# Deferred sums in the seven-product blocks, gate rows behind them, and an early start of the last projection in a two-layer trunk kernel

## The chip, the core and the metric

The kernel runs on one core of one Trainium2 chip. The metric is the time of one execution in microseconds (us). Before the change it is 1751.2 us, the median of three runs (1747.75 to 1752.89).

The core has a matrix engine (TensorE, PE in the rows), a vector engine (VectorE, DVE), a scalar engine (ScalarE, ACT), a general engine (GpSimd, POOL), and a queue engine that issues transfers (SyncE, SP). Each works through its own list of instructions in order and waits where an operand or a buffer isn't ready.

## What is computed

Two layers over 512 tokens of 2048 features, all in float32. Layer 0 is an attention layer; the change touches nothing in it. Layer 1 is an mLSTM with 8 heads (q and k of 128, v of 256 features a head):

```python
proj = x @ w_in
qk, v, o, gates, z = jnp.split(proj, [o1, o2, o3, o4], axis=-1)
qk = silu(causal_depthwise_conv(qk, conv_w, conv_b))     # 4 taps
q, k = jnp.split(qk, 2, axis=-1)
i_pre, f_pre = split(gates + gate_b)                      # 8 + 8 columns
cell = mlstm_chunkwise(q, k, v, i_pre, f_pre)             # decays from cumulated log-sigmoid(f), running maximum
cell = rmsnorm(cell, head_norm)                           # per head
y = (sigmoid(o) * cell * silu(z)) @ w_out
x = layernorm(ALPHA * x + y, ln_w, ln_b)
```

## The kernel before

Every float32 product is three products of rounded parts: hi·hi, hi·lo and lo·hi (`mm3`). A weight tile comes by a transfer of SyncE into `raw` (a ring of 3), ScalarE casts it to `whi` (L169), VectorE subtracts to get `wlo` (L170). A matmul covers 128 x 128 x 512; 24 of them use up one pair of K tiles. So VectorE must end one subtraction for each such group, or TensorE waits.

The order is written by a small planner in the program itself: `tick`, called between groups of products, runs tasks (generators) whose due time on a clock of counted TensorE work has passed; a `yield n` puts a task off by n us. `finish` drains a task at once. The framework then fixes the order on each engine.

Layer 1 goes through these stages:

- `values_out` for columns 0 to 511 of v: tokens 0 and 1, then 2 and 3 while the rest of the layer's input is still being transposed ("late").
- `gates` (L740 onward): one load of the 16 gate columns, 32 products, then `gate_rows`: a run of small VectorE operations on 8 partitions (log-sigmoid as a series, a reciprocal, running sums and maxima, L761 to L795), and after a pause a transpose of the rows. Their results are the cells' decays (`self.R` in DRAM) and gate columns (`self.gt`).
- `values_out` for columns 1536 to 2047, and beside it the task `mlstm_combos` (L917, with L281 to L284 and splits): eight bursts that build the sums of input tiles which the seven-product blocks need.
- Five `quad` blocks: each computes a 2 x 2 block product with seven products instead of eight. Phase 1 takes products q1 and q5 (96 matmuls), phase 2 q7, q6, q3 (144), phase 3 q2 and q4 (96); weights of several products are sums (L348, L360, L362, L381). After phase 2 ten sums over results follow (L368 to L374), after phase 3 four (L386). The first quad gives v columns 512 to 1535, each other one the columns of o and z of two heads, of which sigmoid(o)·silu(z) goes to `ascr` in DRAM. Phases alternate between the two sets of four accumulators, `acc` and `ps`.
- Four pairs of heads: v of the pair (`v_block`), the q and k products (`gemm_b`), convolution and SiLU (`conv_silu`, L808 to L811), and two `cell` tasks of one head each: decay loads on GpSimd's queue, exp, mask, S = k·q, scaled and split; products with v; root mean square (with L262 on GpSimd); scaling (L878); transposes; the result goes to `gscr` in DRAM, for the last two heads it stays.
- `out_proj` with w_out: blocks of 512 columns, residual tiles (`resid1`: `n1` times LayerNorm row plus bias on GpSimd, L1071 and L1072), statistics, and `finish1`, the last LayerNorm. One cell runs at a time (`width` 1), beside whatever products come.

A cell takes up to 13 tiles of the `t` pool (16), and the residual tiles of a block 4 more of it.

Of the kernel before, what the change touches and what calls it, by code (L numbers as in the profile page):

```python
# [2 lines left out]

# [13 lines left out]
P = 128  # L17
# [63 lines left out]
class Kern:  # L81
    def __init__(self, ctx, tc):
# [12 lines left out]
        self.banks = self.ps, self.acc  # L95

# [132 lines left out]
    def gemm_a(self, w, col0, x, toks, last=1):  # L229


        nk = len(x)
        out = {tb: self.acc() for tb in toks}
        units = []
        for k0 in range(0, nk, 2):
# [14 lines left out]
            for i, tb in enumerate(toks):  # L250
                s = slice(tb * P, (tb + 1) * P)
                for kk, (xh, xl), wk in units:
                    self.mm3(out[tb], (xh[:, s], xl[:, s]), wk, kk == 0, kk == nk - 1)
                self.tick()
# [20 lines left out]
    def combos(self, te, to, alloc):  # L275
# [14 lines left out]
        return out  # L290

    def quad(self, w, c0, c1, x, S, done):
# [48 lines left out]
        for i in range(0, n, 2):  # L341
# [8 lines left out]
            mul(q5, so, 1, i, taken2(t[-1]))  # L350
        e1, e5 = two(self.t), two(self.t)
# [356 lines left out]
    def out_proj(self, w_out, g, resid, finish, last=1):  # L708
# [7 lines left out]
        blocks = [((0, 1, 2, 3), 0), ((0, 1, 2, 3), 1)] + [(p, c) for p in ((0, 1), (2, 3)) for c in (2, 3)]  # L716
        for toks, cb in blocks:
            for tb in toks:
                t = r[tb, cb] = self.t()
                resid(tb, cb, t)  # L720
            out = self.gemm_a(w_out, cb * 512, g, toks, last if toks[0] == 2 and cb == 3 else 1)
            for tb in toks:
                t = r[tb, cb]
                nc.vector.scalar_tensor_tensor(t, t, ALPHA, out[tb], op0=ALU.mult, op1=ALU.add)
                nc.vector.bn_stats(stats[tb][:, cb], t)
            if cb == 3:
                moments = {}
                for tb in toks:
                    mv, a = self.small(2, 4), self.small()
                    nc.vector.bn_aggr(mv, stats[tb])  # L730
                    nc.vector.tensor_scalar(a, mv[:, 1:2], EPS, None, ALU.add)
# [389 lines left out]
```

## Time and profile before

| what | us |
|---|---|
| median of three runs | 1751.2 |
| profiled execution | 1744.94 |
| its span (first to last instruction) | 1743.2 |
| TensorE busy | 1629.5 (93%) |
| VectorE busy | 1095.0 (63%) |
| ScalarE busy | 742.3 (43%) |
| GpSimd busy | 151.2 (9%) |

The mean clock granted to TensorE in this execution was 0.979 of full speed. By stretch of the span:

| stretch, us | what runs | TensorE busy, us |
|---|---|---|
| 722 to 770 | first values, late transposes | 48.00 of 48 |
| 770 to 782 | gates | 9.48 of 12 |
| 782 to 825 | last values, gate rows, combos | 43.00 of 43 |
| 825 to 850 | first quad's head | 4.91 of 25 |
| 848 to 1271 | five quads | 393.51 of 423 |
| 1271 to 1471 | pair projections with cells 0 to 3 | 199.66 of 200 |
| 1471 to 1589 | cells 4 to 7, first block of the last projection | 79.41 of 118 |
| 1589 to 1743 | rest of the last projection, LayerNorm | 138.51 of 154 |

A busy share is an average over stages with different limits: where TensorE is full, another engine's work costs nothing; where it isn't, the row says which wait ended last. Busy time at a lower clock counts as busy, so the granted clock stands beside it.

### The profile page before, as it was taken

How to read it: one execution, taken by the hardware profiler on the slowest of the kernel's cores; microseconds unless marked ns; L12 is line 12 of the kernel's file. 1: busy time of each engine (PE TensorE's matmuls, PEld its weight loads, DVE VectorE, ACT ScalarE, POOL GpSimd, SP SyncE). 2: the span in 40 equal slices, each digit the busy share in tenths (PEclk: the TensorE clock that was granted, in tenths of full speed). 3: DMA queues.
4: the chain of work that ended last, by engine and by line, in shares of the span. 5: the costliest groups of instructions: out<-in, count | busy, mean ns of one | idle time of the engine just before them, and what ended most of it. 6: DMA issues, size and time to landing. Idle time of an engine off the chain costs nothing.

```text
span 1743.2 us, 20540 instructions
## 1 busy us (share of the span) xinstructions
PE 1629.5 (93%) x7466; PEld 1338.5 (77%) x7466; DVE 1095.0 (63%) x1880; ACT 742.3 (43%) x1178; POOL 151.2 (9%) x238
## 2 busy tenths in 40 slices
PE   8999999999999999999599998998899998679996
PEld 7888888888888888778477776876688887457875
DVE  3374222777778346859876877786756564555477
ACT  3343223545555224452434444544545564653232
POOL 1000000000000001101000000000110111324300
PEclk9999999999999999999799999999999999789999
DMA  7333333322222546664455475547655743456454
GB/s 207 107 96 97 97 97 85 91 63 66 73 70 88 157 145 218 214 174 87 135 133 161 121 149 108 175 120 145 135 149 123 145 122 121 122 159 207 155 193 169
DMA packets 172134, 230.05 MB, mean 132 GB/s; under 512 B 23593, under 2 KB 93321, under 8 KB 172033
## 3 DMA queue, kind: packets, MB, share of 16 engines
q1 hardware_dynamic: 157872, 195.72, 41.9%
q0 software_dynamic: 7248, 20.44, 3.9%
q10 hardware_dynamic: 6912, 12.59, 2.4%
q8 instruction: 58, 0.95, 0.2%
q14 instruction: 44, 0.35, 0.1%
HBM read 206.51 MB, written 19.96 MB: 130 GB/s over the span
## 4 chain that ended last, share of the span: by engine, by line
PE 68%; DVE 14%; DMA 12%; ACT 3%; issue 3%; POOL 0%; SPq 0%; DVEq 0%; POOLq 0%; ACTq 0%
PE acc L204 56%; PE ps L204 10%; DMA raw<-in_ml_w_in_dram 8%; DVE wlo L170 5%; PE ps L201 2%; DMA raw<-in_ml_w_out_dram 2%; ACT whi L169 1%; DVE raw L360 1%; DVE t L381 1%; DVE h L170 1%; DMA e<-in_ml_w_in_dram 1%; DVE e L917 0%; DMA e<-vscr 0%; ACT h L169 0%; DVE t L372 0%
## 5 line engine op out<-in xcount | busy, mean ns | idle before, releaser
L170 DVE TENSOR_TENSOR wlo<-raw,whi 128x1024 fp32r<-128x1024 f32 (+1 forms) x311 | 377.3, 1215 | 324.3 <-ACT whi L169 311.0
L169 ACT CAST whi<-raw 128x1024 fp32r<-128x1024 f32 (+1 forms) x315 | 324.3, 1030 | 570.6 <-PE acc L204 376.9
L204 PE MATMUL acc<-whi,h 128*128 128x512 f32 x1656 | 533.3, 396 | 15.2 <-ACT whi L169 8.6
L204 PE MATMUL acc<-h,whi 128*128 128x512 f32 x1536 | 473.7, 393 | 2.5 <-DVE whi L170 2.5
L204 PEld LDWEIGHTS acc<-whi,h 128*128 128x128 f32 x1656 | 313.2, 189 | 81.0 <-ACT whi L169 10.0
L204 PE MATMUL acc<-wlo,h 128*128 128x512 f32 x828 | 327.0, 395 | 14.1 <-DVE wlo L170 14.1
L204 PEld LDWEIGHTS acc<-h,whi 128*128 128x128 f32 x1536 | 286.8, 189 | 60.7 <-DVE whi L170 2.9
L204 PE MATMUL acc<-h,wlo 128*128 128x512 f32 x736 | 287.5, 391 | 0.0
L204 PEld LDWEIGHTS acc<-wlo,h 128*128 128x128 f32 x828 | 157.0, 190 | 51.7 <-DVE wlo L170 20.9
L204 PEld LDWEIGHTS acc<-h,wlo 128*128 128x128 f32 x736 | 138.4, 188 | 29.5
L204 PE MATMUL ps<-whi,h 128*128 128x512 f32 x488 | 156.3, 392 | 0.0
L204 PE MATMUL ps<-wlo,h 128*128 128x512 f32 x244 | 97.1, 398 | 12.6 <-DVE wlo L170 12.6
L204 PEld LDWEIGHTS ps<-whi,h 128*128 128x128 f32 x488 | 92.1, 189 | 19.1
L169 ACT CAST whi<-t 128x512 fp32r<-128x512 f32 x120 | 69.1, 617 | 59.6 <-PE ps L204 34.4
L204 PE MATMUL acc<-whi,v 128*128 128x512 f32 x248 | 84.4, 399 | 0.0
L201 PE MATMUL ps<-ident,t 128*128 128x128 f32 x352 | 60.1, 288 | 22.6 <-ACT t L878 16.9
L170 DVE TENSOR_TENSOR wlo<-t,whi 128x512 fp32r<-128x512 f32 x120 | 77.9, 685 | 1.1 <-ACT whi L169 0.9
L201 PEld LDWEIGHTS ps<-ident,t 128*128 128x128 f32 x352 | 46.0, 147 | 38.1 <-ACT t L878 19.8
L204 PEld LDWEIGHTS ps<-wlo,h 128*128 128x128 f32 x244 | 45.9, 188 | 28.2 <-DVE wlo L170 19.0
L204 PE MATMUL ps<-h,h 128*128 128x128 f32 (+3 forms) x288 | 62.0, 328 | 0.1
L685 ACT ACTIVATE t<-ps,s 128x128 f32<-128x128 f32 (+3 forms) x64 | 33.7, 527 | 65.2 <-DVE s L684 65.1
L204 PE MATMUL ps<-whi,v 128*128 128x512 f32 x120 | 42.4, 409 | 20.1 <-ACT whi L169 20.1
(209 smaller groups left out, 1740.0 us busy)
## 6 DMA issues: line engine op xcount, KB each, us to landing
raw<-in_ml_w_in_dram SPq DMA_DIRECT2D x136, 512.0 KB, 4.9
raw<-in_mla_w_in_dram SPq DMA_DIRECT2D x48, 512.0 KB, 3.8
raw<-in_mla_w_out_dram SPq DMA_DIRECT2D x48, 512.0 KB, 3.8
raw<-in_ml_w_out_dram SPq DMA_DIRECT2D x48, 512.0 KB, 4.5
e<-in_ml_w_in_dram SPq DMA_DIRECT2D x40, 256.0 KB, 4.8
t<-in_x_dram SPq DMA_DIRECT2D x16, 256.0 KB, 6.5
raw<-in_mla_w_kvb_dram SPq DMA_DIRECT2D x16, 256.0 KB, 3.3
raw<-in_mla_w_kvb_dram SPq DMA_DIRECT2D x32, 128.0 KB, 2.4
```

What stands on the lines that cost most here:

```text
L169: a = self.nc.scalar.copy(hi, src)
L170: b = self.nc.vector.tensor_tensor(lo, src, hi.bitcast(F32), op=ALU.subtract)
L201: self.nc.tensor.transpose(out, in_, ident)
L204: self.nc.tensor.matmul(out, lhsT, rhs, start=start, stop=stop)
L360: V.tensor_tensor(w12, w12, w22, op=ALU.add)
L381: V.tensor_tensor(t[i // 2][j], t[i // 2][j], half(w21, j), op=ALU.add)
L685: nc.scalar.activation(pt[bi], s[:, :n], AF.Exp, bias=b, scale=scale, accum_out=tot)
```

## The change

Four edits. Of the sums over results in `quad`, all but the first two (L368) aren't issued where they were but put into a list, `self.pending`; `some(2)` takes two entries after each step of phases 1 and 3, so those of phase 2 fall into the first three steps of phase 3, those of phase 3 into the first two steps of the next quad's phase 1. `gates` and its rows are called behind the five quads, and a cell starts only when the rows are done. `v_block` is called for each head, within the cell, with hi and lo in one tile. `out_proj` goes over blocks 0 and 1 twice: first K tiles 0 to 11 (heads 0 to 5), then 12 to 15, added with four more evictions a block; the residual tiles of these blocks come from `h`, and its residual and LayerNorm loads are issued from SyncE instead of ScalarE. Pauses in `cell` are longer.

```diff
+    def some(self, n):
+
+        for _ in range(min(n, len(self.pending))):
+            self.pending.pop(0)()
...
             mul(q1, xe, 0, i, taken(w11))
             mul(q5, so, 1, i, taken2(t[-1]))
+            self.some(2)
...
-        for m in range(2):
+
+        def sums(m):
             V.tensor_tensor(e5[m], e5[m], u[m], op=ALU.subtract)
             V.tensor_tensor(u[m], u[m], q7[m], op=ALU.add)
+
+        def upper(m):
             V.tensor_tensor(c12[m], e5[m], q3[m], op=ALU.add)
             done(m, 1, c12[m])
+
+        def lower(m):
             V.tensor_tensor(e5[m], e5[m], q7[m], op=ALU.subtract)
             done(2 + m, 1, e5[m])
+        self.pending += [partial(f, m) for f in (sums, upper, lower) for m in range(2)]
...
             mul(q2, xo, 0, i, taken(w21))
             mul(q4, xo, 1, i, taken2(t[i // 2]))
-        for c, q, v in ((0, q2, e1), (2, q4, u)):
-            for m in range(2):
-                V.tensor_tensor(v[m], v[m], q[m], op=ALU.add)
-                done(c + m, 0, v[m])
+            self.some(2)
+
+        def left(tb, v, q):
+            V.tensor_tensor(v, v, q, op=ALU.add)
+            done(tb, 0, v)
+
+        self.pending += [partial(left, c + m, v[m], q[m]) for c, v, q in ((0, e1, q2), (2, u, q4)) for m in range(2)]
...
-    def out_proj(self, w_out, g, resid, finish, last=1):
+    def out_proj(self, w_out, g, resid, finish, last=1, early=0):
...
+        def block(toks, cb, ks=(0, KT), last=1):
+            for tb in toks if ks[0] == 0 else ():
+                t = r[tb, cb] = self.h() if early and cb < 2 else self.t()
                 resid(tb, cb, t)
...
+                nc.vector.scalar_tensor_tensor(t, t, 1.0 if ks[0] else ALPHA, out[tb], op0=ALU.mult, op1=ALU.add)
+                if ks[1] == KT:
+                    nc.vector.bn_stats(stats[tb][:, cb], t)
+
+        every = (0, 1, 2, 3)
+        for ks in ((0, early), (early, KT)) if early else ((0, KT),):
+            for cb in range(2):
+                block(every, cb, ks)
...
-    def cell(self, hd, q, k, vs, ascr, out, gscr):
+    def cell(self, hd, q, k, vscr, ascr, out, gscr, rows):
...
+        while not rows.done:
+            yield 1.0
...
-        yield 5.0
+        vs = self.v_block(vscr, hd)
+        yield 6.0
...
-            yield 1.5 if sb < 3 else 1.0
+            yield 1.5 if sb < 3 else 2.5
...
-            yield 1.5
+            yield 2.0
...
-        yield 6.0
+        yield 11.0
...
-    def v_block(self, vscr, pair):
+    def v_block(self, vscr, hd):
+
         res = []
...
+        for i in range(2):
+            raw = self.e().rearrange("p (b c) -> p b c", c=DV)
+            src = vscr[2 * i * P : (2 * i + 2) * P, hd * DV : (hd + 1) * DV]
+            self.nc.sync.dma_start(raw, src.rearrange("(b p) c -> p b c", p=P))
...
-        rows = self.start(self.gates(w_in, x))
         self.values_out(w_in, x, 1536, (0, 1, 2, 3), vscr)
         self.finish(combos)
...
-        self.finish(rows)
...
+        self.some(len(self.pending))
+        rows = self.start(self.gates(w_in, x))
         tasks = []
         for pair in range(H1 // 2):
-            vs = self.v_block(vscr, pair)
...
     def resid1(tb, cb, t):
-        nc.scalar.dma_start(t, rows(n1, tb, cb))
+        nc.sync.dma_start(t, rows(n1, tb, cb))
...
-    for t in K.out_proj(ml_w_out[0], Ahead([g1(i) for i in range(KT)], 2), resid1, finish1, 5):
+    for t in K.out_proj(ml_w_out[0], Ahead([g1(i) for i in range(KT)], 2), resid1, finish1, 5, 12):
```

The order on the engines at three places. First VectorE's list where the values end and quad 1 begins. Before, the last combo (L917, L281 to L284, and L170 into an `h` tile) ends right ahead of quad 1's first weight sum (L348):

```order
L170 TENSOR_TENSOR h_7338<-e_7329,h_7337 128x512
L170 TENSOR_TENSOR h_7342<-e_7330,h_7341 128x512
L917 TENSOR_TENSOR e_7346<-h_6310,h_6311 128x512
L281 TENSOR_TENSOR e_7346<-e_7345,e_7346 128x256
L282 TENSOR_TENSOR e_7345<-e_7345 128x256
L283 TENSOR_TENSOR e_7345<-e_7346,e_7345 128x256
L284 TENSOR_TENSOR e_7346<-e_7346,e_7345 128x256
L170 TENSOR_TENSOR h_7354<-e_7345,h_7353 128x512
L348 TENSOR_TENSOR t_7367<-raw_7365,e_7369 128x512
```

After, the lines have other numbers (L947 for L917, L283 to L286, L172 for L170, L355 for L348); the rows are the last combo, the last weight splits of the values and quad 1's first:

```order
L285 TENSOR_TENSOR e_7237<-e_7238,e_7237 128x256
L286 TENSOR_TENSOR e_7238<-e_7238,e_7237 128x256
L172 TENSOR_TENSOR wlo_7119<-raw_7117,whi_7118 128x1024
L172 TENSOR_TENSOR h_7246<-e_7237,h_7245 128x512
L172 TENSOR_TENSOR h_7250<-e_7238,h_7249 128x512
L172 TENSOR_TENSOR wlo_7149<-raw_7147,whi_7148 128x1024
L172 TENSOR_TENSOR wlo_7268<-raw_7257,whi_7267 128x1024
L355 TENSOR_TENSOR t_7259<-raw_7257,e_7261 128x512
L355 TENSOR_TENSOR t_7260<-raw_7257,e_7264 128x512
```

The last weight splits of the values (the first and third `wlo` of them) now stand behind combos, and no combo stands behind the last. Second, VectorE's list at the head of a quad's phase 3 (quad 1). Before, the sums L368 to L374 come as a block, and the `wlo` rows are halves of the next weight:

```order
L370 TENSOR_TENSOR t_7543<-t_7543,t_7783 128x512
L370 TENSOR_TENSOR t_7544<-t_7544,t_7784 128x512
L371 TENSOR_TENSOR t_7783<-t_7783,acc_7549 128x512
L372 TENSOR_TENSOR t_7785<-t_7543,acc_7553 128x512
L371 TENSOR_TENSOR t_7784<-t_7784,acc_7550 128x512
L374 TENSOR_TENSOR t_7543<-t_7543,acc_7549 128x512
L372 TENSOR_TENSOR t_7786<-t_7544,acc_7554 128x512
L170 TENSOR_TENSOR wlo_7826<-t_7367,whi_7825 128x512
```

After, with L379, L380 and L383 for L370, L371 and L372:

```order
L172 TENSOR_TENSOR wlo_7706<-t_7259,whi_7705 128x512
L172 TENSOR_TENSOR wlo_7706<-t_7260,whi_7705 128x512
L379 TENSOR_TENSOR t_7435<-t_7435,t_7675 128x512
L379 TENSOR_TENSOR t_7436<-t_7436,t_7676 128x512
L380 TENSOR_TENSOR t_7675<-t_7675,acc_7441 128x512
L380 TENSOR_TENSOR t_7676<-t_7676,acc_7442 128x512
L172 TENSOR_TENSOR wlo_7732<-raw_7727,whi_7731 128x1024
L383 TENSOR_TENSOR t_7677<-t_7435,acc_7445 128x512
L172 TENSOR_TENSOR wlo_7748<-t_7303,whi_7747 128x512
L172 TENSOR_TENSOR wlo_7748<-t_7304,whi_7747 128x512
L383 TENSOR_TENSOR t_7678<-t_7436,acc_7446 128x512
```

The sums now stand in pairs between the splits. Third, TensorE's list where the last pair projections have ended. Before, these rows are the end of the drained cell 4 (its products with v and its transposes) and the last projection's first product, 60 rows behind the last projection of a pair:

```order
L204 MATMUL ps_12523<-v_11236,t_12392 128x258
L204 MATMUL ps_12523<-v_11237,t_12389 128x256
L201 MATMUL ps_12555<-ident,t_12478 128x128
L201 MATMUL ps_12561<-ident,t_12478 128x128
L201 MATMUL ps_12555<-ident,t_12478 128x128
L201 MATMUL ps_12561<-ident,t_12478 128x128
L201 MATMUL ps_12555<-ident,t_12479 128x128
L201 MATMUL ps_12561<-ident,t_12479 128x128
L201 MATMUL ps_12555<-ident,t_12479 128x128
L201 MATMUL ps_12561<-ident,t_12479 128x128
L204 MATMUL acc_12263<-whi_12268,h_12273 128x512
```

After, the rows are cell 3's S, its first products with v and the last projection's first (25 rows behind):

```order
L206 MATMUL ps_12253<-h_10894,h_11132 128x128
L206 MATMUL ps_12263<-v_12140,t_12206 128x258
L206 MATMUL ps_12263<-v_12140,t_12209 128x258
L206 MATMUL ps_12263<-v_12140,t_12206 128x256
L206 MATMUL ps_12274<-v_12140,t_12206 128x258
L206 MATMUL ps_12274<-v_12140,t_12209 128x258
L206 MATMUL ps_12274<-v_12140,t_12206 128x256
L206 MATMUL ps_12274<-v_12144,t_12207 128x258
L206 MATMUL ps_12274<-v_12144,t_12210 128x258
L206 MATMUL ps_12274<-v_12144,t_12207 128x256
L206 MATMUL acc_12067<-whi_12072,h_12077 128x512
```

The first product of the last projection moved from behind a whole cell into the middle of one.

## Rows read from the trace of the kernel before

**Rows 1.** Busy time and share of the span, on the page.

```profile
PE 1629.5 (93%) x7466; PEld 1338.5 (77%) x7466; DVE 1095.0 (63%) x1880; ACT 742.3 (43%) x1178; POOL 151.2 (9%) x238
```

**Rows 2.** Windows: busy us (instructions) by engine, clock, DMA share, GB/s.

```profile
722.00:770.00 48.00, 48.00 (x227) 39.01 (x225) 33.64 (x63) 24.89 (x40) 9.67 (x14) 1.00 0.71 209
...
782.00:825.00 43.00, 43.00 (x191) 35.41 (x189) 40.29 (x62) 13.31 (x18) 3.61 (x7) 1.00 0.47 92
825.00:850.00 25.00, 4.91 (x20) 3.27 (x19) 22.94 (x45) 9.11 (x16) 1.62 (x3) 0.68 0.18 58
```

**Rows 3.** TensorE's timeline: start, us, instruction, [idle before <-releaser].

```profile
772.70 1.65 PE L204 MATMUL acc<-h,whi 128*128 128x512 f32 x3 [2.52 <-DVE whi L170]
...
848.79 0.79 PE L204 MATMUL ps<-whi,v 128*128 128x512 f32 x1 [20.09 <-ACT whi L169]
...
854.50 0.39 PE L204 MATMUL ps<-wlo,v 128*128 128x512 f32 x1
```

**Rows 4.** VectorE's timeline: a gate row; quad 1's first sum.

```profile
787.37 3.34 DVE L771 RECIPROCAL e<-e 8x512 f32<-8x512 f32 x1
...
847.35 0.68 DVE L348 TENSOR_TENSOR t<-raw,e 128x512 f32<-128x512 f32 x1
```

**Rows 5.** VectorE by line, 780 to 850: count | busy, mean | idle before.

```profile
L170 DVE TENSOR_TENSOR wlo<-raw,whi 128x1024 fp32r<-128x1024 f32 x9 | 10.8, 1205 | 4.2 <-ACT whi L169 4.2
L917 DVE TENSOR_TENSOR e<-h,h 128x512 f32<-128x512 f32 x16 | 10.3, 680 | 0.0
L170 DVE TENSOR_TENSOR h<-e,h 128x512 fp32r<-128x512 f32 x10 | 6.5, 688 | 1.1 <-ACT h L169 1.1
...
L284 DVE TENSOR_TENSOR e<-e,e 128x256 f32<-128x256 f32 x8 | 3.4, 425 | 0.3
```

**Rows 6.** Windows: five phases 3 summed, four phases 1 summed, one phase 2.

```profile
sum 114.90, PE 108.23 PEld 87.25 DVE 106.33 ACT 60.93 POOL 7.73; mean PE 21.65 PEld 17.45 DVE 21.27 ACT 12.19 POOL 1.55
...
sum 93.90, PE 87.93 PEld 70.20 DVE 71.66 ACT 45.42 POOL 8.64; mean PE 21.98 PEld 17.55 DVE 17.91 ACT 11.35 POOL 2.16
...
1031.00:1074.00 43.00, 36.28 (x153) 27.79 (x151) 23.40 (x29) 14.80 (x20) 0.00 (x0) 1.00 0.53 98
```

**Rows 7.** VectorE's timeline at the head of quad 1's phase 3.

```profile
903.82 1.28 DVE L368 TENSOR_TENSOR t<-ps,t 128x512 f32<-128x512 f32 x2
...
909.21 0.68 DVE L170 TENSOR_TENSOR wlo<-t,whi 128x512 fp32r<-128x512 f32 x1
```

**Rows 8.** TensorE's timeline at the same place.

```profile
909.95 0.51 PE L204 MATMUL ps<-wlo,h 128*128 128x512 f32 x1 [0.92 <-DVE wlo L170]
```

**Rows 9.** Windows of the tail, its first 35 us and the whole.

```profile
1471.00:1506.00 35.00, 13.91 (x59) 11.48 (x60) 20.22 (x51) 26.44 (x49) 5.60 (x13) 0.66 0.29 81
...
1471.00:1589.00 118.00, 79.41 (x377) 64.30 (x378) 65.51 (x162) 70.56 (x140) 28.75 (x42) 0.84 0.45 137
```

**Rows 10.** TensorE's waits, 1471 to 1506.5: total us, times, longest.

```profile
PE ps L201 <- ACT t L878: 13.3, 4, 8.2
```

**Rows 11.** TensorE's timeline in the tail.

```profile
1505.52 0.79 PE L204 MATMUL acc<-whi,h 128*128 128x512 f32 x1 [4.89 <-ACT h L169]
...
1563.67 2.07 PE L204 MATMUL acc<-whi,h 128*128 128x512 f32 x4 [8.00 <-ACT whi L169]
```

**Rows 12.** Chain that ended last, an unbroken stretch: start, us, count.

```profile
1588.49 91.57 PE acc L204 x396
```

**Rows 13.** Window of the first pair's projections.

```profile
1271.00:1315.00 44.00, 44.00 (x196) 36.46 (x195) 20.92 (x25) 16.79 (x21) 4.47 (x9) 1.00 0.60 152
```

**Rows 14.** DMA issues, 1271 to 1590: count, KB, median us to landing.

```profile
t<-ascr SPq DMA_DIRECT2D x14, 256.0 KB, 6.2
e<-vscr SPq DMA_DIRECT2D x12, 256.0 KB, 4.7
```

**Rows 15.** GpSimd's timeline in the tail.

```profile
1507.70 2.51 POOL L1071 TENSOR_TENSOR t<-t,h 128x512 f32<-128x512 f32 x2 [5.34 <-DMA h<-in_ln_w_dram]
...
1539.67 0.10 POOL L907 MEMSET v<- 128x4 f32 x1 [19.64 <-PE ps L204]
```

More of the change, by code (lines that the diff above doesn't have):

```diff
@@ L2 @@
 from contextlib import ExitStack
+from functools import partial
 import concourse.bass as bass
@@ L227, in gemm_b, with gemm_a @@
         return out
-    def gemm_a(self, w, col0, x, toks, last=1):
-        nk = len(x)
+    def gemm_a(self, w, col0, x, toks, last=1, ks=(0, KT)):
+        k1, nk = ks
         out = {tb: self.acc() for tb in toks}
         units = []
-        for k0 in range(0, nk, 2):
+        for k0 in range(k1, nk, 2):
             src = w[k0 * P : (k0 + 2) * P, col0 : col0 + 512]
@@ L252, in gemm_a @@
                 for kk, (xh, xl), wk in units:
[L253 removed]
+                    self.mm3(out[tb], (xh[:, s], xl[:, s]), wk, kk == k1, kk == nk - 1)
                 self.tick()
@@ L715, in out_proj @@
         stats = {tb: self.const.tile([P, 4, 6], F32, tag="bn", bufs=4, name=self.name("bn")) for tb in range(NTB)}
[L716 to L719, printed above, removed]
+        def block(toks, cb, ks=(0, KT), last=1):
+            for tb in toks if ks[0] == 0 else ():
+                t = r[tb, cb] = self.h() if early and cb < 2 else self.t()
                 resid(tb, cb, t)
-            out = self.gemm_a(w_out, cb * 512, g, toks, last if toks[0] == 2 and cb == 3 else 1)
+            out = self.gemm_a(w_out, cb * 512, g, toks, last, ks)
             for tb in toks:
                 t = r[tb, cb]
[L724 to L731, printed above, removed]
-                    moments[tb] = mv[:, 0:1], self.rsqrt_small(a)
-                tasks.append(self.add(finish(toks, r, moments)))
+                nc.vector.scalar_tensor_tensor(t, t, 1.0 if ks[0] else ALPHA, out[tb], op0=ALU.mult, op1=ALU.add)
[5 more added lines that the diff above has]
+                block(every, cb, ks)
+        for toks in ((0, 1), (2, 3)):
+            block(toks, 2)
+            block(toks, 3, last=last if toks[0] else 1)
+            moments = {}
+            for tb in toks:
+                mv, a = self.small(2, 4), self.small()
+                nc.vector.bn_aggr(mv, stats[tb])
+                nc.vector.tensor_scalar(a, mv[:, 1:2], EPS, None, ALU.add)
+                moments[tb] = mv[:, 0:1], self.rsqrt_small(a)
+            tasks.append(self.add(finish(toks, r, moments)))
         return tasks
@@ L937, in mlstm, with gate @@
                   lambda tb, col, t: self.value_out(tb, 512 + 512 * col, t, vscr))
-        self.finish(rows)
         for pair in range(H1 // 2):
             z = {}
-            def gate(tb, col, t):
+            def gate(tb, col, t, pair=pair, z=z):
                 if col:
@@ L963, in mlstm @@
                 out = [self.h() if hd < H1 - 1 else self.e() for _ in range(2)]
-                cell = self.cell(hd, q[j], k[j], vs, ascr, out, gscr if pair < 3 else None)
+                cell = self.cell(hd, q[j], k[j], vscr, ascr, out, gscr if pair < 3 else None, rows)
                 t = self.add(cell, 0.0 if j else 4.0)
```

33 lines of the change are left out of this document (16 added, 17 removed).

## The prediction

> **What bounds the kernel now.** I read the page's busy shares first, then the list of who waited for whom on TensorE, then the windows by stage, then the timelines where TensorE stands still. TensorE is busy for 1629.5 us, 93% of the span [rows 1], so only the places where it stands still or runs at half clock can give anything: the change adds and removes no product. Three places matter.
>
> First, the stretch from 825 to 850 us: TensorE is busy for 4.91 of 25 us [rows 2]. One wait of 20.09 us stands there, ended by a weight cast at 848.79 [rows 3]. That product is the first quad's q5, whose weights need the sum of L348, which VectorE does at 847.35, after the last split of the combos [rows 4]. VectorE is what is late: it is busy for 40.29 of the 43 us before and 22.94 of these 25 [rows 2]. Between 780 and 850 it does the eight combos: 10.3 us for L917, some 11.0 for the splits (16 at 0.688), 3.4 for each of L281 to L284, together 34.9 us; nine weight splits take 10.8 [rows 5]. The rest of its 63 us, some 17.5, is chiefly gate rows (one reciprocal on 8 partitions takes 3.34 us [rows 4]), and they are queued ahead of the combos.
>
> Second, the quads. In the five stretches of phase 3 TensorE is idle for 114.9 - 108.2 = 6.7 us, in four of phase 1 for 93.9 - 87.9 = 6.0 [rows 6]. VectorE is busy there for 106.3 of 114.9 and 71.7 of 93.9 us. In phase 3 the sums L368 to L374 run as a block from 903.82, the next half of a weight split comes at 909.21 [rows 7], and TensorE waits 0.92 us for it at 909.95 [rows 8].
>
> Third, the tail, from 1471 to 1589 us, in which the last four cells run with the first block of the last projection: TensorE is busy for 79.41 of 118 us at a granted clock of 0.84; the first 35 us hold 21.1 of the 38.6 idle ones, at 0.66 [rows 9]. There the transposes of a cell wait 13.3 us for L878, and the first product of the last projection 4.9 us, until 1505.52 [rows 10, 11], since its accumulators belong to the last pair's convolutions until then.
>
> **The change part by part.** *Gate rows behind the quads.* The 17.5 us of gate rows leave VectorE's queue ahead of the combos. By the order of the instructions the combos now stand between the weight splits from the second half of the first values on, and the last is done before the last weight split of the values ahead of quad 1. VectorE was busy for 33.64 of the 48 us from 722 to 770 [rows 2]; from 722 to 825 it then has 33.6 + 34.9 + 10.8, 79 of 103 us. That fits. The 20.1 us go. So does the restart: the 12 matmuls from 848.79 to 854.50 take 5.71 us [rows 3] where 396 in a row take 91.57, or 0.231 each, 2.8 for 12 [rows 12]: 2.9 us more. Late next is the weight of quad 1's phase 1, which in quads 2 to 5 costs 1.5 us on average [rows 6]; and the combos, in bursts of over 4 us between splits, may hold up a product or two in the late stage, 0 to 4 us; I take 1. 20.1 + 2.9 - 1.5 - 1 = 20.5, from 15 (all 4, and a worse first phase) to 23.
>
> The clock granted over 825 to 850 was 0.68 of full speed [rows 2], so part of that stretch ran at the lower of the two levels (1.2 GHz), and the restart belongs to the gap. The Trainium skill says of this (TensorE: Matmul & The Clock Gate, What's actually happening) that throttled is the state at rest and that activity releases it. The trace agrees: 0.68 stands right after 43 us of TensorE without a break at 1.00. By the rule the 2.9 us go with the gap; were the slow start quad 1's own, the term would be 17.6.
>
> *The gates' own place.* Before, TensorE waited 2.52 us at 772.70 for their weights [rows 3]. They are now asked for inside the last phase 3, so I expect no wait: 2.5 gained. The 17.5 us of gate rows land on the first pair's projections, where VectorE is busy for 20.92 of 44 us with TensorE at 44.00 [rows 13]; 38 of 44 fits, but each weight split then waits behind up to 3.34 us. I set 2.5 against that: 0, from -3 to +2.5. The cells now wait for the rows; the first cell's products start some 30 matmuls later, with other products in their place.
>
> *Sums put off.* Eight of the ten sums leave the block for three steps of 24 matmuls. The work stays and VectorE is near full in phase 3, so not all 6.7 us can go; the 0.92 us wait in each of five quads is 4.6. The four left-hand sums move out of the head of the next phase 1 into its first two steps, a few tenths. I take 5; 2 if VectorE's throughput keeps most of it, 9 if phase 3 becomes clean and phase 1 gains a third. The slow phase 2 of quads 3 and 5 (43 us with 36.28 busy [rows 6]) stays: the same weights through the same ring.
>
> *The tail.* By the order, the last projection's first product now stands 25 matmuls after the end of the pair projections (60 before), since the last pair's k convolutions no longer follow a drained cell; 24 products of it stand between the steps of cells 3 to 6, and 288 instead of 192 can be used, as blocks 0 and 1 run over 12 K tiles. Cell 3 was finished inside the pair projections before and is not now; the 41 products that stood with it there move behind (9.4 us at 0.231), while cell 7 now runs between products; I set these against each other. The residual tiles leave the `t` pool, so two cells can overlap. Their loads and those of the LayerNorm rows go from ScalarE's queue, which saves it their issue, to the sync queue, where they wait for free `h` tiles with the next w_out and gscr loads behind them; a v load waits there for its `e` tile, so for an earlier cell's v splits. Who waits for that is TensorE, for w_out. I price this at nothing, since one w_out and three gscr loads are asked for ahead of them, and at 12 us in rival (b) if that cover is gone. The 4.9 us go (the cause is gone), and of the 13.3 us I take half, since the chain of a cell from its mean square over L262 to L878 is as long as before and only what stands beside it changes: 11.5, less 0.5 for eight more evictions: 11. Low: 3 (the 4.9 less one v load late); high: 21, all idle time of these 35 us. The wait of 8.00 us at 1563.67 for w_out behind a gscr round trip [rows 11] can stay.
>
> Each head now loads its own v in pieces of 1 KB instead of 2. The gate loads (`t<-ascr`) have 1 KB pieces already and land after 6.2 us, the v loads after 4.7 [rows 14]: 1.5 us later where it shows. The Trainium skill speaks against such pieces (DMA: Bandwidth & Descriptors, Why small descriptors are slow): a fixed cost of about 3 cycles a packet beside one per 32 bytes. By that, an estimate from its figures, 1 KB pieces cost 4.5% more, 0.2 us of 4.7. I keep the row's 1.5, once, in the low end.
>
> **Sum.** 20.5 + 0 + 5 + 11 = 36.5 us. The profiled execution took 1744.94 (span 1743.2), 6.3 below the median of 1751.2. On it the sum gives 1708.4; on the median 1714.7. I forecast 1714.
>
> **The rivals.** (a) VectorE becomes the bound of the late stage: combos hold weight splits back one by one. For it: bursts of over 4 us against a split wanted about every 5.5 us (24 products at 0.231). Against: 79 of 103 us. If six of the eight bursts cost 2 us, 12 us return: 1727. Chance 0.12. (b) The tail gives nothing: eight residual sums of the first block on GpSimd took from 1507.70 to 1520.0 (1539.67 less 19.64 of idle [rows 15]) and now stand ahead of cell 4's decay loads in its queue; on the sync queue the residual and v loads stand ahead of w_out's. One such hold-up of 12 us eats the 11: 1726. Chance 0.20. (c) The tail's first 35 us fill up wholly: 10 more, 1705. Chance 0.17. (d) The change doesn't do what it says: the gate rows only move the stall to the first pair; 3.34 us behind each of four splits, 13 us: 1728. Chance 0.05. (e) Slower: with 24 products (5.5 us) between drained cells' steps, a chain of GpSimd and DMA serves one cell at a time: decay load, exp, split, products, rsqrt, transposes. Before, four drained cells had 38.6 us idle [rows 9], 9.6 each. Five cells are drained partly now; the gains ahead of the tail are 25.5, so the kernel is slower from 38.6 + 25.5 = 64 us idle, 12.8 a cell. At the 19.64 us for which GpSimd once stood idle before a cell [rows 15] it is 98 us idle: 34 slower than before, 1785. Against it: 96 more products to stand beside them and the free `t` tiles. Chance 0.03.
>
> **How the numbers follow.** The forecast has 0.43; rivals (a) to (d) 0.54, all faster; (e) 0.03. A difference of 0.3%, 5 us, is about what a measurement of this kernel can tell from no change. Faster by more has 0.95, 0.02 of the rivals' chance going to within 0.3% (two of them together); slower 0.03. The range takes in (a) to (d) with the bounds: 1696 to 1731.
>
> **What the profile will show.** Right: no TensorE wait over 3 us between 770 and 850; quad 1's phase 1 near 23 us; phase 3 with under 1 us idle and sums in pairs between weight splits; gate rows beside the first pair with TensorE full; the first `raw<-in_ml_w_out` product within 15 us of the end of the pair projections, and the tail's 118 us near 107. Wrong: weight splits waiting behind L917's successors; GpSimd's residual sums ahead of a late decay load; a clock near 0.66 again in the tail.

## The result

The changed kernel takes 1699.55 us (median of four runs, 1697.65 to 1700.4) against 1752.05 before in the same comparison (four runs, 1747.75 to 1754.93): ratio 0.9701, 95% interval 0.9678 to 0.9723, so 3% less, 52 us. Its profiled execution took 1698.93 us (span 1697.2). The forecast was 1714, in a range of 1696 to 1731, so the measured time lies 3.5 us above the range's low end.

The page of the changed kernel (busy us, share of the span, instructions), beside [rows 1]:

```profile
PE 1625.4 (96%) x7466; PEld 1338.7 (79%) x7466; DVE 1100.6 (65%) x1904; ACT 740.7 (44%) x1192; POOL 151.7 (9%) x254
```

TensorE is busy for about as long as before (1625.4 against 1629.5 us) in a span that is 46 us shorter: some 42 us of the gain are idle time that is gone. Windows of the changed kernel (length, busy us by engine, granted clock, DMA share, GB/s) at the late stage, quad 1's phase 1, the gates behind the quads, the first pair and the tail, which answer to [rows 2, 9, 13]:

```profile
722.00:772.00 50.00, 48.85 (x229) 39.54 (x229) 45.91 (x87) 29.03 (x48) 7.76 (x12) 1.00 0.74 212
...
816.00:838.00 22.00, 22.00 (x99) 18.12 (x98) 17.65 (x24) 12.01 (x18) 0.88 (x2) 1.00 0.52 163
...
1239.00:1283.00 44.00, 44.00 (x196) 36.45 (x195) 37.10 (x50) 18.48 (x22) 5.25 (x10) 1.00 0.56 157
1433.00:1571.00 138.00, 113.64 (x546) 93.33 (x545) 85.10 (x206) 73.97 (x161) 43.98 (x61) 0.90 0.63 198
```

```profile
1231.90:1239.20 7.30, 7.30 (x34) 6.04 (x33) 5.85 (x9) 3.27 (x4) 2.16 (x4) 1.00 0.58 143
```

In the kernel before, the same products of the gates, behind the wait for their weights:

```profile
772.60:781.60 9.00, 8.90 (x33) 7.26 (x34) 2.70 (x4) 2.89 (x4) 1.07 (x2) 0.82 0.71 189
```

In quad 1's phase 1 TensorE has no gap any more; the late stage, in which VectorE is now busy for 45.91 of 50 us (33.64 of 48 before), loses a little (one wait of 1.1 us for a weight split; another of 1.5 us stands in quad 1's phase 2); the gates and the first pair lose nothing, though VectorE rises to 37.10 of 44 us there. The sums over the five phases 3, beside [rows 6]:

```profile
sum 110.00, PE 110.00 PEld 91.10 DVE 104.14 ACT 63.02 POOL 5.14; mean PE 22.00 PEld 18.22 DVE 20.83 ACT 12.60 POOL 1.03
```

TensorE is busy for all 110 us. VectorE's timeline at the head of the first of them (L379, L380 and L383 are before's L370 to L372), beside [rows 7]:

```profile
873.39 1.28 DVE L172 TENSOR_TENSOR wlo<-t,whi 128x512 fp32r<-128x512 f32 x2
874.59 1.28 DVE L379 TENSOR_TENSOR t<-t,t 128x512 f32<-128x512 f32 x2
875.80 1.28 DVE L380 TENSOR_TENSOR t<-t,acc 128x512 f32<-128x512 f32 x2
876.99 1.22 DVE L172 TENSOR_TENSOR wlo<-raw,whi 128x1024 fp32r<-128x1024 f32 x1
878.13 0.68 DVE L383 TENSOR_TENSOR t<-t,acc 128x512 f32<-128x512 f32 x1
```

The next weight split starts at 873.39, ahead of the sums that stood in front of it before, and the one at 876.99 comes between the sums. The tail still idles for 24.4 of 138 us, with more products in it. What TensorE waits for there (total us, times, longest; L905 is before's L878, L878 before's L850, L206 before's L204):

```profile
PE acc L206 <- ACT whi L171: 15.2, 5, 5.9
PE ps L206 <- DVE t L878: 4.9, 3, 3.2
...
PE ps L203 <- ACT t L905: 0.7, 1, 0.7
```

In the tail of before (1471 to 1590) the two largest were:

```profile
PE ps L201 <- ACT t L878: 16.9, 6, 8.2
PE acc L204 <- ACT whi L169: 8.4, 2, 8.0
```

The waits for scaled tiles ahead of the transposes, 16.9 us before, are down to 0.7; those for casts of w_out have grown from 8.4 to 15.2.

Where the 46.0 us between the two spans lie, by the first product of each stage in TensorE's timelines:

| stretch | before, us | after, us | gained |
|---|---|---|---|
| to the end of the late values | 770.0 | 772.6 | -2.5 |
| gates with the wait ahead of them | 11.6 | 7.25 (behind the quads) | 4.3 |
| last values | 44.1 | 43.5 | 0.6 |
| quad 1, phase 1 | 45.23 | 21.87 | 23.4 |
| phases 2 (five) | 189.7 | 191.2 | -1.4 |
| phases 3 (five) | 115.0 | 108.8 | 6.2 |
| phases 1 of quads 2 to 5 | 95.5 | 94.1 | 1.4 |
| pair projections, tail and rest | 472.1 | 458.0 | 14.1 |

In the last line the work that moved from one of its parts into the next cancels: pair projections 199.4 to 193.7, tail 118.0 to 138.2, and a rest of 154.7 to 126.1 that has some 120 matmuls fewer. And of the 2.5 us in the first line 1.0 is older than the change: the product behind a wait of 2.04 us before and of 2.05 after starts at 705.68 before and at 706.69 after, while the combos' first addition comes at 738.80. It goes back to the input's first loads, in layer 0.

### The profile page after: what moved, and what is told of

Its sections match the earlier page's. It is cut to its first block, busy times and chain, and to the rows that moved or that the text cites. A ratio compares the mean times of both kernels' runs of the same rounds, so it can differ in the third digit from the quotient of the medians.

```text
span 1697.2 us, 20582 instructions
## 1 busy us (share of the span) xinstructions
PE 1625.4 (96%) x7466; PEld 1338.7 (79%) x7466; DVE 1100.6 (65%) x1904; ACT 740.7 (44%) x1192; POOL 151.7 (9%) x254
## 4 chain that ended last, share of the span: by engine, by line
PE 70%; DMA 14%; DVE 11%; issue 2%; ACT 2%; POOL 1%; SPq 0%; DVEq 0%; POOLq 0%; ACTq 0%
PE acc L206 58%; PE ps L206 10%; DMA raw<-in_ml_w_in_dram 9%; DVE wlo L172 5%; PE ps L203 2%; DMA raw<-in_ml_w_out_dram 1%; DVE raw L368 1%; ACT whi L171 1%; DMA e<-vscr 1%; DVE t L395 1%; DMA e<-in_ml_w_in_dram 1%; POOL s L264 0%; DMA gscr<-h 0%; DVE t L370 0%; DMA raw<-in_mla_w_out_dram 0%
## 5 line engine op out<-in xcount | busy, mean ns | idle before, releaser
L206 PE MATMUL acc<-whi,h 128*128 128x512 f32 x1656 | 537.8, 398 | 15.6 <-ACT whi L171 15.2
L172 DVE TENSOR_TENSOR wlo<-raw,whi 128x1024 fp32r<-128x1024 f32 (+1 forms) x311 | 377.6, 1216 | 269.0 <-ACT whi L171 254.5
L171 ACT CAST whi<-raw 128x1024 fp32r<-128x1024 f32 (+2 forms) x315 | 324.5, 1030 | 518.0 <-PE acc L206 344.7
L206 PE MATMUL acc<-h,whi 128*128 128x512 f32 x1536 | 471.9, 392 | 0.0
L206 PEld LDWEIGHTS acc<-whi,h 128*128 128x128 f32 x1656 | 315.2, 191 | 81.5 <-ACT whi L171 16.7
L206 PE MATMUL acc<-wlo,h 128*128 128x512 f32 x828 | 329.7, 398 | 12.0 <-DVE wlo L172 11.8
L206 PEld LDWEIGHTS acc<-h,whi 128*128 128x128 f32 x1536 | 286.2, 188 | 58.2 <-issue 1.0
L206 PE MATMUL acc<-h,wlo 128*128 128x512 f32 x736 | 287.4, 390 | 0.0
L206 PEld LDWEIGHTS acc<-wlo,h 128*128 128x128 f32 x828 | 158.0, 191 | 50.3 <-DVE wlo L172 18.7
L206 PEld LDWEIGHTS acc<-h,wlo 128*128 128x128 f32 x736 | 138.5, 188 | 29.5
L206 PE MATMUL ps<-whi,h 128*128 128x512 f32 x488 | 156.5, 392 | 0.0
L206 PEld LDWEIGHTS ps<-whi,h 128*128 128x128 f32 x488 | 92.4, 189 | 19.3
L206 PE MATMUL ps<-wlo,h 128*128 128x512 f32 x244 | 97.0, 397 | 10.2 <-DVE wlo L172 10.2
L171 ACT CAST whi<-t 128x512 fp32r<-128x512 f32 x120 | 68.6, 618 | 59.0 <-PE ps L206 35.3
L206 PE MATMUL acc<-whi,v 128*128 128x512 f32 x248 | 84.7, 400 | 0.0
L172 DVE TENSOR_TENSOR wlo<-t,whi 128x512 fp32r<-128x512 f32 x120 | 77.4, 685 | 9.0 <-ACT whi L171 9.0
L206 PEld LDWEIGHTS ps<-wlo,h 128*128 128x128 f32 x244 | 46.2, 189 | 23.8 <-DVE wlo L172 14.4
L206 PE MATMUL ps<-h,h 128*128 128x128 f32 (+3 forms) x288 | 60.3, 323 | 4.1 <-DVE t L878 4.1
L370 DVE TENSOR_TENSOR t<-t,raw 128x512 f32<-128x512 f32 x40 | 26.6, 688 | 49.2 <-DMA raw<-in_ml_w_in_dram 49.2
```

What stands on the lines that cost most here:

```text
L171: a = self.nc.scalar.copy(hi, src)
L172: b = self.nc.vector.tensor_tensor(lo, src, hi.bitcast(F32), op=ALU.subtract)
L206: self.nc.tensor.matmul(out, lhsT, rhs, start=start, stop=stop)
L370: V.tensor_tensor(t[i // 2][j], t[i // 2][j], half(w22, j), op=ALU.add)
```

## The experiments

Each ratio is to the kernel before, timed beside it on the same chip; its medians there were 1748.4 to 1749.8 us. Where a run is set against the changed kernel, its ratio is compared with 0.9701, and its median with 1699.55 where both are given.

**One part alone.** Three kernels each take one part of the change into the kernel before.

e1, the gates:

```diff
-        rows = self.start(self.gates(w_in, x))
         self.values_out(w_in, x, 1536, (0, 1, 2, 3), vscr)
...
-        self.finish(rows)
...
+        rows = self.start(self.gates(w_in, x))
         tasks = []
...
+        while not rows.done:
+            yield 1.0
```

> The kernel before with one edit of the change: gates and their rows are called behind the quads, the cells wait for the rows. My theory (the gate rows keep VectorE from the combos, and quad 1 waits for those): the 20.1 us gap, the 2.9 us restart and the 2.5 us wait for the gates' weights go, some 2 us come back in the late stage: 22 to 26 us faster than before (ratio 0.985 to 0.987). Rival (the parts only work together, since the end of the quads just moves the wait to the first pair or to the tail): under 12 us (0.993 or more).

Measured: 1724.37 us, ratio 0.9858 (0.9841 to 0.9875), 24 us faster.

```profile
816.00:838.00 22.00, 22.00 (x98) 18.14 (x97) 17.66 (x24) 12.19 (x19) 0.54 (x1) 1.00 0.55 164
```

Quad 1's phase 1 is clean in this kernel too. The part stands by itself. (As in the change, the pause ahead of the rows' transpose is 50 instead of 40 here.)

e2, the sums: the edits of `quad`, `some` and `pending` and nothing else.

> The kernel before with only the sums put off. My theory (a block of sums makes a weight split late at the head of each phase 3): each of the five phases 3 goes from 23.0 to 21.8 us, 6 us in all (ratio 0.9965), nothing elsewhere. Rival (VectorE's throughput is the limit there): phases 3 stay near 22.7 and the whole within 2 us (0.999).

Measured: 1743.62 us, ratio 0.9976 (0.9965 to 0.9987), 4 to 5 us faster where 6 were expected, and clear of the rival's 2. The windows of the five phases 3, summed:

```profile
sum 109.80, PE 108.78 PEld 89.16 DVE 105.79 ACT 62.02 POOL 5.07; mean PE 21.76 PEld 17.83 DVE 21.16 ACT 12.40 POOL 1.01
```

TensorE is busy for 108.78 of 109.8 us, while VectorE is as busy as before (105.79; 106.33 in [rows 6]) in 5 us less. So it was the order and not VectorE's throughput in these phases: the rival falls.

e3, the cells and the last projection: `v_block` for each head, the longer pauses, `early=12`, residual tiles from `h`, the last LayerNorm's rows in `v` tiles, loads by SyncE; gates and sums as before.

> The kernel before with only the edits of cells and last projection: v for each head, longer pauses, 12 K tiles of blocks 0 and 1 first, residual tiles from h and loads by SyncE. My theory (the tail's gain is its own): 12 to 16 us faster (0.991 to 0.993). Rival (it needs the gates' shift, which changes where the cells meet the projections): under 6 us (0.997 or more).

Measured: 1730.88 us, ratio 0.9898 (0.9883 to 0.9912), 17 to 18 us faster: its own, and a bit more than expected. The three parts alone give 24.0, 4.8 and 17.5 us, 46 together, where the change as a whole gives 52; the intervals of the ratios leave room for either.

**What the gate rows did to quad 1.** My prediction put the gap of quad 1 down to VectorE's time: 17.5 us of gate rows ahead of the combos. But the combos of before start only at 804.31, although VectorE had 14 us idle between 722 and 770 [rows 2]:

```profile
803.19 1.19 DVE L792 TENSOR_TENSOR_SCAN e<-e,h 8x512 f32<-8x512 f32 x1
804.31 0.65 DVE L917 TENSOR_TENSOR e<-h,h 128x512 f32<-128x512 f32 x1
```

L792 is the first running sum of the gate rows, the last of their operations to take new tiles of `e`. Gate rows and combos both take their work tiles from `e`, a pool of three, and the combos are written behind the rows. e4 leaves everything in its place and gives the rows tiles of `t`:

```diff
-        tmp, gi, lf = self.e(), self.h(), self.h()
+        tmp, gi, lf = self.t(), self.h(), self.h()
...
-        f = self.e()
+        f = self.t()
...
-        a, s = self.e(), self.e()
+        a, s = self.t(), self.t()
...
-        m, cum, one = self.h(), self.e(), self.e()
+        m, cum, one = self.h(), self.t(), self.t()
```

> The kernel before, gates and rows at their old place, but the rows' six work tiles come from the pool t instead of e, the pool of three from which the combos take theirs too. No work of VectorE is saved or moved behind the quads. Theory of the prediction (VectorE's time: 17.5 us of gate rows ahead of the combos make them late): the gap in quad 1's first phase stays at 14 us or more, ratio 0.996 or more. Rival (the ring of e tiles: combos written after the gate rows cannot start before the rows give their tiles back, although VectorE has idle time earlier): combos start in the late stage, VectorE fits 97 us of work into the 103 up to quad 1, and the gap falls to under 6 us: 17 to 22 us faster (0.987 to 0.990).

Measured: 1728.59 us, ratio 0.9882 (0.9864 to 0.99), 20 us faster, with six tiles from another pool and no work moved behind the quads. VectorE's timeline of this kernel, the first additions of the combos (L917), the rows' reciprocal, the last addition and quad 1's first sum:

```profile
737.60 0.68 DVE L917 TENSOR_TENSOR e<-h,h 128x512 f32<-128x512 f32 x1
...
738.54 1.29 DVE L917 TENSOR_TENSOR e<-h,h 128x512 f32<-128x512 f32 x2
...
789.36 3.34 DVE L771 RECIPROCAL t<-t 8x512 f32<-8x512 f32 x1
...
827.54 0.68 DVE L917 TENSOR_TENSOR e<-h,h 128x512 f32<-128x512 f32 x1
...
830.83 0.69 DVE L348 TENSOR_TENSOR t<-raw,e 128x512 f32<-128x512 f32 x1 [0.51 <-DMA e<-in_ml_w_in_dram]
```

and TensorE's, ahead of the gates and at quad 1's q5:

```profile
774.54 5.76 PE L204 MATMUL acc<-h,whi 128*128 128x512 f32 x17 [3.74 <-DVE whi L170]
...
832.28 0.74 PE L204 MATMUL ps<-whi,v 128*128 128x512 f32 x2 [1.58 <-ACT whi L169]
```

The combos begin at 737.60, nine of the 16 additions come ahead of the gate rows' reciprocal, and the 20.09 us at q5 [rows 3] are 1.58. VectorE carries both in time. The rival holds: the ring of three tiles made the gap, not the work. Beside e4, e1 saves the wait for the gates' weights (3.74 us here), the slower products behind it, and 4.3 us of phase 1 (26.1 against 21.9 us), 8 us in all by the first pair's projections (1246.4 against 1254.5 us in the two traces); its tail loses them again. By medians e1 is 4 us faster, with intervals that overlap; of the two profiled executions e4's is the shorter (1722.4 against 1723.5 us). What the gates' new place gives beyond new tiles isn't settled.

**What the tail's gain is made of.** Three kernels undo one thing each in the changed kernel (ratio 0.9701).

e5, no early blocks:

```diff
-    for t in K.out_proj(ml_w_out[0], Ahead([g1(i) for i in range(KT)], 2), resid1, finish1, 5, 12):
+    for t in K.out_proj(ml_w_out[0], Ahead([g1(i) for i in range(KT)], 2), resid1, finish1, 5):
```

> The changed kernel with the last projection as before: no split of blocks 0 and 1 into K tiles 0 to 11 and 12 to 15, and so their residual tiles from t again; everything else stays changed. My theory (the early blocks are what fills the tail): most of the tail's gain goes, 10 to 17 us slower than the changed kernel (ratio to before 0.976 to 0.980). Rival (the longer pauses, v for each head and loads by SyncE are what counts): under 4 us slower (0.9725 or less).

Measured: 1703.3 us, ratio 0.9734 (0.9708 to 0.9759): 4 to 6 us slower than the changed kernel by medians and ratio, with intervals that overlap, between the two theories. The early blocks are the smaller part.

e6, v for each pair again (`v_block` of before, called ahead of the q projection, the cell reading its half):

```diff
-        vs = self.v_block(vscr, hd)
+        vs, c0 = vscr, (hd % 2) * 258
...
         for pair in range(H1 // 2):
+            vs = self.v_block(vscr, pair)
             q_ps = self.gemm_b(w_in, 0, pair * 256, x)
```

> The changed kernel with v loaded and split for each pair again, ahead of its q projection, instead of within the cell of each head. My theory (v for each head only serves to free v tiles, its 1 KB pieces cost next to nothing): within 4 us of the changed kernel (0.968 to 0.9725). Rival (v in the cell is what keeps loads off the path, as a load of 6.7 us stood in the chain of waits of the kernel before at the head of the tail): 5 us or more slower (0.973 or more).

Measured: 1721.79 us, ratio 0.9841 (0.981 to 0.9871): 22 to 24 us slower than the changed kernel, more than the tail's whole gain. TensorE's timeline in its tail:

```profile
1458.20 2.15 PE L203 MATMUL ps<-ident,t 128*128 128x128 f32 x8 [8.76 <-ACT t L905]
1480.41 0.80 PE L206 MATMUL acc<-whi,h 128*128 128x512 f32 x1 [20.06 <-ACT h L171]
```

and what SyncE's queue waits for between 1425 and 1485 (L932 is the v load, L1085 the read back from gscr):

```profile
SPq L1085 <- DVE h L172: 23.1, 1, 23.1
SPq L932 <- DVE v L172: 18.2, 1, 18.2
```

The last projection's first product comes at 1480.41, after 20.06 us (1443.77 in the changed kernel). A load of the last pair's v waits 18.2 us in SyncE's queue for splits of v to give its work tile back; a pair's v takes eight of the 12 v tiles, so two pairs don't fit, and what fills them waits until the products of a cell before are done. GpSimd's timeline shows that wait at the fill of ones, and the chain that ended last goes from there over a decay load:

```profile
1447.36 0.10 POOL L934 MEMSET v<- 128x4 f32 x1 [18.27 <-PE ps L206]
...
1449.21 7.28 DMA t<-decay
```

Behind that load the chain goes through ScalarE's exp and the last pair's convolutions to 1480. My theory, that this edit is neutral, falls. The edit changes two things at once, how many v tiles a load needs and where in the program it stands; they were not separated.

e7, the old pauses:

```diff
-        yield 6.0
+        yield 5.0
...
-            yield 1.5 if sb < 3 else 2.5
+            yield 1.5 if sb < 3 else 1.0
...
-            yield 2.0
+            yield 1.5
...
-        yield 11.0
+        yield 6.0
```

> The changed kernel with the cell's old pauses (5, 1.0, 1.5 and 6 instead of 6, 2.5, 2.0 and 11), so each cell's steps stand closer together in the order. My theory (the pauses set which cells end inside the pair projections, and what stands in the tail is the same amount of work): within 4 us of the changed kernel (0.968 to 0.9725). Rival (the longer pauses are what keeps TensorE from waiting for the cell's own chain from mean square to scaled tiles, 16.9 us of waits before and 0.7 after): 6 us or more slower (0.9735 or more).

Measured: 1697.41 us, ratio 0.9699 (0.9673 to 0.9725): no difference. The pauses move the waits (L905 takes 10.8 us in its tail, casts of w_out 8.8) without changing their sum.

e9 takes v for each head alone into the kernel before (`v_block` and the cell's use of it, as in the change).

> The kernel before with one edit: v loaded and split for each head within its cell. Theory after the run with v for each pair (24 us slower than the changed kernel): v for each head is the largest part of the tail's gain, since a pair's eight v tiles take up most of the ring of 12 and the loads and one-fills of the last pair wait for cells, with other work behind them in two queues: 8 to 17 us faster than before (0.990 to 0.995). Rival (v for each pair only hurts together with the early blocks and the later LayerNorm rows in v tiles): within 3 us of before (0.998 to 1.002).

Measured: 1738.07 us, ratio 0.9946 (0.9928 to 0.9965), 9 to 11 us faster. Its first product of the last projection:

```profile
1488.61 0.79 PE L204 MATMUL acc<-whi,h 128*128 128x512 f32 x1 [1.73 <-ACT h L169]
...
1501.93 2.94 PE L204 MATMUL ps<-v,t 128*128 128x258 f32 x12 [5.78 <-DVE t L851]
```

It comes 15 us after the pair projections' last product (1473.3), where before took 35 (1470.5 to 1505.52 [rows 11]). The theory holds. The parts of the tail don't add up one by one: v for each head alone gives 10, the whole 17.5, and the rest without it gives nothing that shows: e6 stands 27 to 28 us below before, where gates and sums alone give 29 together.

e10 asks which queue is the path in before. GpSimd stands 34.27 us at a fill of ones until a v tile is free, with decay loads behind it (GpSimd's timeline of before):

```profile
1465.43 0.10 POOL L907 MEMSET v<- 128x4 f32 x1 [34.27 <-PE ps L204]
1465.92 0.60 POOL L825 DMA_DIRECT2D t<-decay  x1 [0.38 <-issue]
```

The edit:

```diff
-            self.nc.gpsimd.memset(view(hi.bitcast(F32))[:, :, DV:258], 1.0)
+            self.nc.scalar.copy(view(hi)[:, :, DV:258], self.ones[:, 64:68].rearrange("p (h c) -> p h c", c=2))
```

> The kernel before with one edit: the columns of ones in the v tiles are written by ScalarE instead of GpSimd. In the trace of before GpSimd stands 34.27 us at one of these fills until a v tile is free, with the decay loads of the next cell behind it in its queue, and ScalarE has that cell's exp ahead of the last pair's convolutions. Theory (this queue is the path by which v for each pair holds up the tail): the decay loads go out earlier, 5 to 12 us faster than before (0.993 to 0.997). Rival (SyncE's v loads or the order on ScalarE are the path): within 3 us (0.998 to 1.002).

Measured: 1745.1 us, ratio 0.9979 (0.9967 to 0.9991), 2 to 6 us by the interval; but in its trace the tail is the same, as TensorE's timeline shows beside [rows 11]:

```profile
1499.85 0.69 PE L201 MATMUL ps<-ident,t 128*128 128x128 f32 x2 [8.19 <-ACT t L878]
...
1507.87 0.79 PE L204 MATMUL acc<-whi,h 128*128 128x512 f32 x1 [4.89 <-ACT h L169]
```

The transposes still wait 8.19 us, the first product of the last projection 4.89. Yet the decay loads did go out earlier, from 1456.08 instead of 1465.92, as GpSimd's timeline shows; what ScalarE waits for ahead of the scaled tiles is now the v load (0.40 us at this cast in before):

```profile
1456.08 0.60 POOL L825 DMA_DIRECT2D t<-decay  x1 [21.58 <-DVE t L170]
...
1475.68 0.62 ACT L169 CAST v<-e 128x512 fp32r<-128x512 f32 x1 [2.99 <-DMA e<-vscr]
```

So GpSimd's queue isn't by itself the path that the theory made of it. The chain of waits of before names the others at the tail's head: a v load of 6.72 us from 1467.31, then ScalarE's cast of it, then L878. Whether SyncE's loads or ScalarE's order (a cell's exp and the casts of v ahead of scaled tiles and the last convolutions) carry the rest was not separated.

**What is left in the tail.** e8 writes the cells' results from ScalarE's queue:

```diff
-                nc.sync.dma_start(gscr[(2 * hd + i) * P : (2 * hd + i + 1) * P], out[i])
+                nc.scalar.dma_start(gscr[(2 * hd + i) * P : (2 * hd + i + 1) * P], out[i])
```

> The changed kernel with the cells' results written to gscr from ScalarE's queue instead of SyncE's, right behind the instruction that makes them. In the tail of the changed kernel SyncE's queue waits 28.6 us in total for those results, with loads of w_out behind, and TensorE waits 15.2 us for casts of w_out. My theory (the queue is what holds w_out back): TensorE's 15.2 us shrink by half or more, 5 to 10 us faster than the changed kernel (0.9645 to 0.9675). Rival (w_out stands behind the read back of the same results, which waits for the write to land, whoever issues it): within 3 us (0.9685 to 0.972).

Measured: 1697.66 us, ratio 0.9701 (0.9674 to 0.9727): no difference; the rival holds. The waits for casts of w_out shrink from 15.2 to 11.9 us in its trace, not by half. e11 asks for w_out one step earlier, in `gemm_a` for the early blocks:

```diff
+        for k0 in range(k1, nk, 2):
+            for kn in (k0, k0 + 2) if ahead else (k0,):
+                if kn < nk and kn not in got:
+                    fetch(kn)
+            wk = got[k0]
```

> The changed kernel with w_out of the early blocks asked for one step ahead, so before the read back of the cells' results that the step after needs. Theory (what is left in the tail, 15.2 us of waits for casts of w_out, comes from w_out's place behind those reads in SyncE's queue): 5 to 12 us faster than the changed kernel (0.963 to 0.967). Rival (the ring of three raw tiles and the cells' own chain set it): within 3 us (0.9685 to 0.972).

Measured: 1690.86 us, ratio 0.9679 (0.9658 to 0.9699). TensorE's waits in its tail:

```profile
PE acc L206 <- ACT h L171: 5.8, 3, 3.2
PE ps L203 <- ACT t L914: 5.2, 3, 2.8
...
PE acc L206 <- DVE h L172: 2.8, 2, 2.5
```

The 15.2 us for casts of w_out are gone, as the theory has it; 8.6 us for the splits of what was read back from gscr (L171 and L172 into `h`) and 5.2 for scaled tiles stand in their place, so only 4 us come out by the ratio (9 by the medians), with intervals that overlap: between theory and rival. e12 adds e8's edit to e11:

> The changed kernel with w_out of the early blocks asked for one step ahead (as in the run before) and, besides, the cells' results written to gscr from ScalarE's queue. In the run before TensorE's waits for casts of w_out had gone and waits for the read back of the results (5.8 + 2.8 us, ScalarE's and VectorE's splits of them) stood in their place. Theory (the round trip through gscr is what is late next, and SyncE's queue, which waits 29.7 us for results there, delays it): another 2 to 6 us, ratio to before 0.964 to 0.967. Rival (the write already goes out as soon as the result is there, whichever queue issues it): the same as the run before, 0.967 to 0.969.

Measured: 1695.34 us, ratio 0.9693 (0.9668 to 0.9717): no further gain. In its trace, TensorE's waits in the tail for what was read back are down from 8.6 to 1.5 us, as the theory has it, but those for scaled tiles rise from 5.2 to 8.4:

```profile
PE ps L203 <- ACT t L914: 8.4, 4, 4.3
...
PE acc L206 <- ACT h L171: 1.2, 2, 0.8
PE acc L206 <- DVE h L172: 0.3, 1, 0.3
```

Both are the fastest kernels of the study by their medians, and both beat before clearly; against the changed kernel the gain, 4 to 9 us for e11 and 1 to 4 for e12 by ratio and medians, is not shown, since the intervals overlap.

## Why the prediction was right, point by point

The sign, the three places and the range held; the sum was short, 36.5 us where the two spans differ by 46.0. The range's low end, 1696, is every term at its best (23, 2.5, 9 and 21 off 1751.2), and the measured time is close to it: the mechanism of the first gap and the edit credited in the tail were partly wrong, and the number came out all the same.

- **Signs.** Those named for being right came: no wait over 3 us from 770 to 850, phases 3 without idle time, TensorE full beside the gate rows, the last projection's first product 10.9 us after the pair projections.
- **Basis.** 6 of the 14.5 us by which the forecast was high come from no term. I added 6.3 us to the profiled time, as before's profiled execution (1744.94) lies below its median. The changed kernel's lies 0.6 below its own. The runs of before spread from 1743 to 1755 over all measurements, those of the changed kernel from 1697.65 to 1700.4; why was not tested.
- **Gap at quad 1: 20.5, measured 23.4 less 1.5.** The 20.1 us and the restart went. Phase 1 then lost nothing (21.87 us) where I took off 1.5. The bursts of combos cost some 1.5 us in the late stage (the 2.5 of the table less the 1.0 that stood before them), where I took 1 in a range of 0 to 4. The failing step is the cause: I read the gate rows as late work because "they are queued ahead of the combos" and put the gap down to VectorE's time, where e4 shows the pool of three tiles. Their 17.5 us were a remainder, too; by their own lines between 780 and 850 they add up to some 21. The same change removes both causes, so that the number came out was in part luck; a reader of the prediction would have thought that the rows' work must leave this stretch, and a change of tiles in six places that moves none of it gives 20 of the 24 us.
- **The gates' own place: 0, measured 4.3.** The wait of 2.52 us went, and 1.7 more, since 32 products behind that wait ran at a granted clock of 0.82 and took 9.0 us, and take 7.3 at 1.00 now. I had priced such a restart at quad 1 but not here. The Trainium skill (TensorE: Matmul & The Clock Gate, What's actually happening) has activity release the throttle; the two clocks agree with it. The 2.5 us set against it on the first pair did not come: VectorE's load there, 37.10 of 44 us, is what was worked out (38), and TensorE stayed full.
- **Sums: 5, measured 6.2 in phases 3.** Right in place and cause; all of the idle time went, where I doubted VectorE's throughput. Phases 1 gave 1.4 and phases 2 took 1.4.
- **Tail: 11, measured 14.1.** Inside the range, with the wrong edit credited. "The 4.9 us go (the cause is gone)" was right, yet the cause goes by v for each head, which I had entered as a cost of up to 1.5 us; e6 prices it at 22 to 24 us within the change and e9 at 10 alone. The early blocks, of which I expected the gain, are worth 4 to 6. The wait of 8.00 us for w_out that "can stay" came back as five pieces that add to 15.2.
- **The pieces of 1 KB.** v loads between 1239 and 1571 land after 5.3 us in the changed kernel, gate loads after 5.8, beside 4.7 and 6.2 [rows 14]: 0.6 us more for v, where I kept 1.5 in the low end; what stands beside the loads differs too, and their price was not tested alone. The Trainium skill's figure (DMA: Bandwidth & Descriptors, Why small descriptors are slow) gives 0.2 as an estimate, less than the 0.6.
- **Rivals.** (a) came in with some 1.5 of its 12 us. (b) came in part: w_out's place in SyncE's queue costs waits of 15.2 us in the tail, which e11 removes, but they did not eat the 11. (d) and (e) didn't come. (c) is nearest: the tail's first 35 us did not fill up wholly (24.8 of 35 us busy, 13.91 before), yet its 1705 is closest to what was measured.

## What to carry to other kernels

Before an idle gap is put down to an engine's load, look whether that engine was idle earlier and what kept the late work from starting there: here it was a pool of three buffers that an unrelated run of small operations used just ahead. Look also at groups of buffers against the size of their ring: here a pair's eight tiles in a ring of 12 kept the next pair's fills waiting (34 us in before, 18 in e6), and loading for one head, within its cell, was worth more than the early start of the next stage. On an engine that is 95% busy the order can still decide: the same sums spread between weight splits, instead of in a block, removed TensorE's stalls in phases 3.

## What the runs showed of the hardware

TensorE ran without a gap through five phases of 22 us each while VectorE fed it and was itself busy for 104.14 of 110 us. And in these rows the price of an operation on VectorE goes by its length and not by its partitions: one on 8 partitions by 512 (L776) took 678 ns in before, one on 128 by 512 (L917) 680, one on 128 by 256 (L284) 425 [rows 5]:

```profile
L776 DVE SCALAR_TENSOR_TENSOR h<-h,e 8x512 f32<-8x512 f32 x7 | 4.7, 678 | 0.2
```
